# w_down of a hybrid block on one Trainium2 core: four Strassen pairs, another order of loads and transposes, results added by DMA

## The chip, the cores and the metric

The kernel runs on one core of one Trainium2 chip. The metric is the device time of one execution in microseconds. The weights lie in HBM in fp32; every matrix product runs on TensorE with fp32 operands split into two parts, and VectorE, ScalarE and GpSimd share the rest of the work.

## What is computed

One block of a streaming encoder, batch 1, sequence 256, width 2048, all in float32 (the reference, cut):

```python
u = rms_norm(x, norm_mix_w)
z = u @ w_in                       # HGRN2 q/f/i/out-gate, attention q/k/v, two branch gates
gate_a, gate_b = jnp.split(jax.nn.sigmoid(gates), 2, axis=-1)
merged = gate_a * (y_a @ w_branch_a) + gate_b * (y_b @ w_branch_b)
h = x + merged @ w_out             # w_out 2048 x 2048
u = rms_norm(h, norm_mlp_w)
h = h + jnp.square(jax.nn.relu(u @ w_up)) @ w_down     # w_up 2048 x 8192, w_down 8192 x 2048
return rms_norm(h, norm_final_w)
```

The recurrence (`y_a`) and the banded attention (`y_b`) come first and are not touched.

## The kernel before

**Products.** An fp32 weight tile is split into wh (ScalarE casts it, L89 in `split`) and wl (VectorE subtracts, L90); the activations are split in the same way beforehand. One k tile of 128 rows is then three matmuls of 128 x 512, hi·wh, hi·wl and lo·wh (`mm3`, L142–145).

**Loads.** SyncE's queue brings two k tiles of 512 columns at a time (`piece`, 512 KB) into a ring of 8 raw buffers. wh and wl have rings of 6 each (`BUFS`, `buf`). A buffer comes free when its last reader is done: a raw one after its last lo subtraction or sum, a wh or wl after its last matmul. Each queue runs in program order, moved by `tc.high_priority`.

**`gemm_s`.** It makes a block of 256 rows by 1024 columns out of 16 k tiles, in four PSUM banks c11, c12, c21, c22 (row half, column half). On r pairs of k tiles (k, k+4) it forms 7 products in place of 8 (Strassen's scheme in Winograd's form); the rest are plain pairs (`plains`, names r0_8, r1_8 and so on: column half and first k tile). Each Strassen pair saves 3 matmuls: 183 at r=3, 186 at r=2, where 192 would be plain. The pieces are W11, W12 (k tiles 0, 1; the two column halves) and W21, W22 (k tiles 4, 5); at r=3 the third pair's four tiles share two buffers X and Y. Sums of weights are made in place in the raw buffers (`add`, L700); sums of activations (S2, S4, S5, S7) are made once by `combos` (L587). A bank that takes over another bank's value starts from a ScalarE copy (L724); `more` (L729) adds or subtracts a token to or from a bank on VectorE. In products whose bank has never been written (`fresh`), a dummy matmul sets it up first (L740). The last pair of column half 1 is held over and runs inside the next product (`late`, `flush`).

**Order.** The products run in a fixed order: ga2, gb0, gb2 (gates, r=3), the branches, wo0 (r=3), wo2 (r=2), then for each of four quarters of the hidden width up{q}0, up{q}2 (r=3, up00 r=2), dn{q}0, dn{q}2 (r=3). Between them the activations are turned: `transpose4` (L106) makes four 128 x 128 transposes into a PSUM buffer (there are two), `split` reads it. A callback `between`, in the middle of the next product, does this for all blocks that are due (`turn`, `turns`, `h_blocks`); in the w_up and w_down products that is 16 transposes in three groups.

**Ends.** `done` gets each finished bank. For w_up it is relu and square on ScalarE (L947, L948). For w_down it is `out_of`: `evict` (L679) adds the bank to h on VectorE. In the last quarter the row sums of squares, the norm (L963–977) and the output DMAs follow; the last product (`tail`) holds three pairs back for column half 1, runs them for m=0, and then for m=1.

Of the kernel before, what the change touches and what calls it, by code (L numbers as in the profile page):

```python
# [16 lines left out]
P = 128  # L17
# [33 lines left out]
def tile_hybrid_block(  # L51
# [534 lines left out]
    def combos(lhs, what, home):  # L586

        a = []
        for m in range(NM):
            for j in range(2):  # L590
                t = tk.tile([P, R, P], F32, name=f"a{m}{j}_{what}", tag="t", bufs=TOK)
                x = lhs[j][:, :R, :, m * P:(m + 1) * P].bitcast(F32)
                nc.vector.tensor_tensor(t, x[:, :, 0, :], x[:, :, 1, :], op=ALU.add)
                a.append(t)
        a11, a12, a21, a22 = a
        s5 = a22
        nc.vector.tensor_tensor(s5, a21, a22, op=ALU.subtract)
        s7 = a21
        nc.vector.tensor_tensor(s7, a11, a21, op=ALU.subtract)
        s2 = a11  # L600
        nc.vector.tensor_tensor(s2, s5, a11, op=ALU.subtract)
        s4 = a12
        nc.vector.tensor_tensor(s4, a12, s2, op=ALU.add)
        made = {}
        for i, s in ((4, s4), (5, s5), (2, s2), (7, s7)):
            t = (tk if home == "a" else xp).tile([P, R, 2, P], F32R, name=f"S{i}_{what}", tag=f"S{i}{home}", bufs=1)
            split(t[:, :, 0, :], t[:, :, 1, :], s)
            made[i] = t
        return made
# [71 lines left out]
    def gemm_s(lhs, S, w, n0, what, done, r=R, kt0=0, between=None, fresh=False, tail=False):  # L681
# [4 lines left out]
        n1 = n0 + NC  # L686
        c = {}
        load = lambda name, *halves: piece(w, f"{what}{name}", *[(n, kt0 + k) for n, k in halves])
        W11 = load("11", (n0, 0), (n0, 1))
        if r == 3:  # L690
            X = load("x", (n0, 2), (n1, 6))
        W22 = load("22", (n1, 4), (n1, 5))
        W12 = load("12", (n1, 0), (n1, 1))
        if r == 3:
            Y = load("y", (n0, 6), (n1, 2))
        W21 = load("21", (n0, 4), (n0, 5))
# [16 lines left out]

        def of(m, jj):
            return lambda k: lhs_of(lhs, k + 4 * jj, m)

        def comb(i):
            return lambda k: [S[i][:, k, u, :] for u in range(2)]

        both = ((0, 0), (1, 1))  # L720
# [5 lines left out]

        def more(i, t, op):
# [4 lines left out]
        p = parts(W11, f"{what}p1")  # L732
        if r == 3:
            px = parts(X, f"{what}px")
        mm("11", of(0, 0), p, *both)
        if r == 3:
            mm("11", of(0, 0), px, (0, 2))
        c["21"] = bank(f"{what}c21")
        if fresh:
            nc.tensor.matmul(c["21"], lhs[0][:, 0, 0, 0:P], lhs[0][:, 0].rearrange("p u t -> p (u t)"), start=True, stop=False, skip_group_check=True)  # L740
        copy(c["21"], "11")
        p = parts(W22, f"{what}p3")
        add(W22[0], W12[0])
        add(W12[0], W11[0])
        mm("12", comb(4), p, *both)
        if r == 3:
            mm("12", comb(4), px, (1, 2))

        p = parts(W12, f"{what}p5")
        mm("22", comb(5), p, *both)  # L750
        if r == 3:
            add(half(X, 1), half(Y, 1))
# [6 lines left out]
        p = parts(W21, f"{what}p2")  # L759
        mm("11", of(0, 1), p, *both)  # L760
        add(W11[0], W22[0])
        flush()

        p = parts(W11, f"{what}p6")
        mm("21", comb(2), p, *both)
        if r == 3:
            add(half(X, 0), half(X, 1))
            px = parts(X, f"{what}px2")
            mm("21", comb(2), px, (0, 2))
        u1 = copy(token(f"u1_{what}"), "21")  # L770

        def plain(n, *ks):
            p = parts(load(f"r{n}_{ks[0]}", *[(n0 + n * NC, k) for k in ks]), f"{what}r{n}_{ks[0]}")
# [14 lines left out]
        left = [(k, k + 1) for k in range(2, KD, 2) if k != 4] if r == 2 else [(3, 7)] + [(k, k + 1) for k in range(8, KD, 2)]  # L788
        plains(1, left[0])
        more("12", u1, ALU.subtract)  # L790
        p = parts(W22, f"{what}p7")
        mm("21", comb(7), p, *both)
        if r == 3:
            mm("21", comb(7), px, (1, 2))
        u2 = copy(token(f"u2_{what}"), "21")
        add(W21[0], W11[0])
        early = left[1][1] // 4 < len(lhs)
        if early:
            plains(1, left[1])
        else:  # L800
            q = plain(0, *left[0])
            q(0)
        more("22", u2, ALU.subtract)
        p = parts(W21, f"{what}p4")
        mm("21", of(1, 1), p, *both)
        if r == 3:
            add(half(Y, 0), half(X, 0))
            mm("21", of(1, 1), parts(Y, f"{what}p4y", 0), (0, 2))
        if not early:
            q(1)  # L810
        if between:
            between()
# [5 lines left out]
        plains(0, *left[0 if early else 1:2])  # L818
        plains(1, *left[2 if early else 1:2])
        for n in range(2):  # L820
            plains(n, *left[2:-3])
        plains(0, *left[max(2, len(left) - 3):])
        end(0)
        if tail:
            held = [plain(1, *ks) for ks in left[-3:]]
            for m in range(NM):
                for p in held:
# [3 lines left out]
        plains(1, *left[-3:-1])  # L831

        def rest():
            plains(1, left[-1])
# [23 lines left out]
    def turn(n):  # L858
        mT.append(new_act(f"m{n}"))
        hi, lo = mT[n][:, :, 0, :], mT[n][:, :, 1, :]  # L860
        for m in range(NM):
            tp = transpose4(ga[n][m], f"m{n}{m}")
            split(hi[:, :, m * P:(m + 1) * P], lo[:, :, m * P:(m + 1) * P], tp)

    for n in range(4):
        for y, w, gate, what in ((ya, w_branch_a, ga[n], "ba"), (yb, w_branch_b, gb[n], "bb")):
# [3 lines left out]
            if what == "ba" and n:  # L870
                turn(n - 1)
# [11 lines left out]
    def h_blocks(n0):  # L883

        for n in (n0, n0 + 1):
            hT.append(new_act(f"h{n}"))
            hi, lo = hT[n][:, :, 0, :], hT[n][:, :, 1, :]
            for m in range(NM):
                t = h1[n][m]
                tp = transpose4(t, f"h{n}{m}")  # L890
                tmp = tk.tile([P, 4, P], F32, name=f"hw_{n}_{m}", tag="t", bufs=TOK)
                nc.vector.tensor_tensor(tmp, tp, bc(wmlp[:, 4 * n:4 * n + 4], 2, P), op=ALU.mult)
                split(hi[:, :, m * P:(m + 1) * P], lo[:, :, m * P:(m + 1) * P], tmp)
                nc.scalar.activation(token(f"hsq_{n}_{m}"), t, AF.Square, accum_out=ssq2[:, m, n:n + 1])
        if not n0:
            Sh.update(combos(hT, "h", "a"))
            return
        ssum2 = small.tile([P, NM], F32, name="ssum2", tag="ssum")
        nc.vector.tensor_reduce(ssum2, ssq2, axis=AX.X, op=ALU.add)
        rsqrt(rstd2, ssum2, D, NM)  # L900

    rstd2 = const.tile([P, NM], F32, name="rstd2")
    for n0 in (0, 2):
        for n in (n0, n0 + 1):
            for m in range(NM):
# [4 lines left out]
               between=lambda: h_blocks(0) if n0 else turn(3))  # L910
# [6 lines left out]
    for qd in range(NQ):  # L917
        last = qd == NQ - 1
        uT = []
        pend = []  # L920

        def turn():

            c, rs = pend.pop(0)
            uT.append(new_act(f"u{qd}{c}"))
            hi, lo = uT[-1][:, :, 0, :], uT[-1][:, :, 1, :]
            for m in range(NM):
# [99 lines left out]
```

## Time and profile before

| | us |
|---|---|
| median of 3 runs | 1425.47 (1424.73 to 1425.62) |
| the profiled execution | 1425.94 |
| its span | 1424.2 |

The profile is of one execution; its span runs from the first to the last instruction, and the execution's own time is 1.7 us longer. Its mean granted TensorE clock is 0.997 of full speed. In the table of windows a row gives a stretch (from:to, length), each engine's busy time and number of instructions in it, the granted clock, the busy share of the DMA engines and their GB/s. A timeline row gives start, duration, engine, line, operation, output and inputs, and in brackets the engine's idle time before it with what ended it. A row of groups ends with count, busy time, mean ns of one, and idle time by releaser. A row of DMA issues gives the count, the size and the median us from issue to landing.

### The profile page before, as it was taken

To read this page: it belongs to the slowest core of one execution; us is meant where nothing else is said; L and a number is where in the kernel's file an instruction comes from. 1 tells how busy PE (TensorE), PEld (TensorE's weight loads), DVE (VectorE), ACT (ScalarE), POOL (GpSimd) and SP (SyncE) were. 2 spreads that over 40 slices of the span, in tenths; PEclk is the share of its full clock that TensorE was granted. 3 is DMA by queue.
4 is the path that set the end of the run, shared out by engine and by line. 5 is a ranking of instruction groups with operands and counts; after the bars stand their busy time and mean duration, and the time that the engine had idled before them with its cause. 6 is when DMAs were issued, how large, how long until landed. Compare 5 with 4: busy or idle time off the path is not lost.

```text
span 1424.2 us, 18429 instructions
## 1 busy us (share of the span) xinstructions
PE 1404.4 (99%) x6629; PEld 1161.3 (82%) x6629; DVE 1153.6 (81%) x1522; ACT 852.8 (60%) x1108; POOL 36.8 (3%) x96
## 2 busy tenths in 40 slices
PE   9999999999999999999999999999999999999997
PEld 7888788878787888888888888888888888888886
DVE  7879887675758885688998988989888998889984
ACT  6766744464556664346656765566556775567753
POOL 2000101010000000000000000000000000000000
PEclk9999999999999999999999999999999999999999
DMA  9664344665556657666654576555576555667542
GB/s 329 221 194 149 130 162 134 189 177 164 166 177 222 202 192 227 197 203 222 207 182 134 192 232 215 181 196 167 188 235 233 183 168 169 236 222 237 179 152 98
DMA packets 122156, 272.89 MB, mean 192 GB/s; under 512 B 10176, under 2 KB 31424, under 8 KB 121680
## 3 DMA queue, kind: packets, MB, share of 16 engines
q1 hardware_dynamic: 119328, 264.80, 55.9%
q0 software_dynamic: 1584, 5.31, 1.4%
q10 hardware_dynamic: 1152, 1.60, 0.3%
q8 instruction: 52, 0.85, 0.2%
q14 instruction: 40, 0.33, 0.1%
HBM read 269.57 MB, written 2.10 MB: 191 GB/s over the span
## 4 chain that ended last, share of the span: by engine, by line
PE 81%; DVE 9%; DMA 4%; ACT 3%; issue 3%; POOL 0%; SPq 0%; POOLq 0%; ACTq 0%; DVEq 0%
PE acc_ak L171 2%; PE acc_aq L171 2%; PE acc_hf L171 2%; PE acc_hq L171 2%; PE ps L395 1%; PE acc_bb L143 1%; PE acc_av L143 1%; PE acc_ba L145 1%; PE acc_ba L144 1%; PE acc_bb L145 1%; PE acc_ba L143 1%; PE acc_av L144 1%; PE acc_bb L144 1%; PE acc_av L145 1%; PE acc_ak L170 1%
## 5 line engine op out<-in xcount | busy, mean ns | idle before, releaser
L171 PE MATMUL acc_hf<-act_x,wh_hf 128*128 128x512 f32 x128 | 47.5, 407 | 0.3 <-DVE wh_hf L89 0.3
L171 PE MATMUL acc_aq<-act_x,wh_aq 128*128 128x512 f32 x128 | 47.7, 407 | 0.0
L171 PE MATMUL acc_hq<-act_x,wh_hq 128*128 128x512 f32 x128 | 45.7, 397 | 0.0
L171 PE MATMUL acc_ak<-act_x,wh_ak 128*128 128x512 f32 x128 | 45.0, 397 | 0.0
L700 DVE TENSOR_TENSOR raw_up<-raw_up,raw_up 128x1024 f32<-128x1024 f32 x32 | 39.1, 1222 | 0.5
L700 DVE TENSOR_TENSOR raw_dn<-raw_dn,raw_dn 128x1024 f32<-128x1024 f32 x32 | 39.1, 1221 | 0.2
L90 DVE TENSOR_TENSOR wl_ga<-raw_ga,wh_ga 128x1024 fp32r<-128x1024 f32 x16 | 19.6, 1225 | 19.6 <-ACT wh_ga L89 17.9
L170 PE MATMUL acc_aq<-act_x,wl_aq 128*128 128x256 f32 x120 | 35.1, 293 | 0.0
L170 PE MATMUL acc_hf<-act_x,wl_hf 128*128 128x256 f32 x120 | 34.3, 286 | 0.0
L90 DVE TENSOR_TENSOR wl_av<-raw_av,wh_av 128x1024 fp32r<-128x1024 f32 x16 | 19.6, 1224 | 18.1 <-ACT wh_av L89 18.1
L170 PE MATMUL acc_ak<-act_x,wl_ak 128*128 128x256 f32 x120 | 33.6, 280 | 0.0
L170 PE MATMUL acc_hq<-act_x,wl_hq 128*128 128x256 f32 x120 | 33.6, 280 | 0.0
L90 DVE TENSOR_TENSOR wl_ba<-raw_ba,wh_ba 128x1024 fp32r<-128x1024 f32 x16 | 19.6, 1225 | 16.6 <-ACT wh_ba L89 16.6
L90 DVE TENSOR_TENSOR wl_bb<-raw_bb,wh_bb 128x1024 fp32r<-128x1024 f32 x16 | 19.6, 1223 | 14.7 <-ACT wh_bb L89 14.7
L89 ACT CAST wh_ba<-raw_ba 128x1024 fp32r<-128x1024 f32 x16 | 16.9, 1054 | 24.3 <-PE acc_ba L145 10.0
L89 ACT CAST wh_bb<-raw_bb 128x1024 fp32r<-128x1024 f32 x16 | 16.9, 1054 | 22.8 <-PE acc_ba L145 12.7
L89 ACT CAST wh_av<-raw_av 128x1024 fp32r<-128x1024 f32 x16 | 16.8, 1053 | 22.0 <-PE acc_av L145 12.4
L90 DVE TENSOR_TENSOR wl_aq<-raw_aq,wh_aq 128x1024 fp32r<-128x1024 f32 x16 | 19.6, 1224 | 12.5 <-ACT wh_aq L89 12.2
L89 ACT CAST wh_aq<-raw_aq 128x1024 fp32r<-128x1024 f32 x16 | 16.8, 1049 | 20.9 <-PE acc_aq L171 8.8
L171 PEld LDWEIGHTS acc_hf<-act_x,wh_hf 128*128 128x128 f32 x128 | 24.1, 188 | 5.7 <-DVE wh_hf L89 0.5
L171 PEld LDWEIGHTS acc_hq<-act_x,wh_hq 128*128 128x128 f32 x128 | 24.0, 188 | 5.4
L171 PEld LDWEIGHTS acc_ak<-act_x,wh_ak 128*128 128x128 f32 x128 | 23.9, 188 | 5.5
(1627 smaller groups left out, 5122.7 us busy)
## 6 DMA issues: line engine op xcount, KB each, us to landing
raw_up<-in_w_up_dram SPq DMA_DIRECT2D x32, 512.0 KB, 5.4
raw_dn<-in_w_down_dram SPq DMA_DIRECT2D x32, 512.0 KB, 5.3
raw_ga<-in_w_in_t_dram SPq DMA_DIRECT2D x20, 512.0 KB, 4.4
raw_hi<-in_w_in_n_dram SPq DMA_DIRECT2D x16, 512.0 KB, 3.9
raw_hg<-in_w_in_n_dram SPq DMA_DIRECT2D x16, 512.0 KB, 3.7
raw_aq<-in_w_in_t_dram SPq DMA_DIRECT2D x16, 512.0 KB, 4.4
raw_ak<-in_w_in_t_dram SPq DMA_DIRECT2D x16, 512.0 KB, 3.8
raw_av<-in_w_in_n_dram SPq DMA_DIRECT2D x16, 512.0 KB, 4.2
```

What stands on the lines that cost most here:

```text
L89: (copy or nc.scalar.copy)(hi, src)
L90: nc.vector.tensor_tensor(lo, src, hi.bitcast(F32), op=ALU.subtract)
L143: nc.tensor.matmul(acc, hi, wh, start=first, stop=False, skip_group_check=True)
L144: nc.tensor.matmul(acc, hi, wl, start=False, stop=False, skip_group_check=True)
L145: nc.tensor.matmul(acc, lo, wh, start=False, stop=last, skip_group_check=True)
L170: nc.tensor.matmul(acc[:, cb, 0:T], wl[:, c], r[:, 0, :], start=False, stop=False)
L171: nc.tensor.matmul(acc[:, cb, :], wh[:, c], r.rearrange("p u t -> p (u t)"), start=kt == 0, stop=kt == nkt - 1)
L395: nc.tensor.matmul(ps[:, m, :], klf[:, a * P:(a + 1) * P], qrf[:, a * 192:(a + 1) * 192], start=True, stop=True)
L700: nc.vector.tensor_tensor(dst, dst, t, op=ALU.add)
```

## The change

1. The w_down products take r=4. The pieces W11, W12, W22 and W21 have two loads each, so that they fill all 8 raw buffers; X and Y fall away there. `combos` gets the fourth tile's sums too (tiles S2m to S7m), and its blocks are copied by ScalarE from the transposes' PSUM buffers in place of being added up from hi and lo.
2. In all `gemm_s` products the loads come in the order of the ring, W11, (X), W12, (Y), W22, W21, and the products in the order c11 from W11, c22 from W12 + W11 with S5, c12 from W22 with S4, then W21. c12 starts from a copy of c22 (`begun`), where a token and a VectorE sum were; W12 is later remade as W22 − W11 (`less`). A `fresh` product has two dummy matmuls, not one. The held-over pair runs after the second product's copy.
3. Transposes are made one block at a time at fixed places (`point`, `steps`, `start`), not together in `between`.
4. In quarters 0 to 2 a w_down bank is copied to a token by ScalarE, and a DMA of GpSimd's queue adds the token to h (24 of 256 KB). The last quarter evicts as before.
5. The last product holds two pairs back for column half 1, and the held-over pair's load is issued at the end of its own product.

In all TensorE has 24 matmuls fewer in w_down and two more in ga2 and gb0; VectorE has 37 instructions fewer, ScalarE 64 more.

```diff
-    def combos(lhs, what, home):
+    def combos(lhs, what, home, blocks=None, n=R):
...
-        for i, s in ((4, s4), (5, s5), (2, s2), (7, s7)):
+        for two in ((5, s5), (4, s4)), ((2, s2), (7, s7)):
+            if n > R:
+                more = tk.tile([P, 2, 2, P], F32R, name=f"S{two[0][0]}m_{what}", tag="t", bufs=TOK)
...
-    def gemm_s(lhs, S, w, n0, what, done, r=R, kt0=0, between=None, fresh=False, tail=False):
+    def gemm_s(lhs, S, w, n0, what, done, r=R, kt0=0, steps=(), start=4, fresh=False, tail=False):
+        def point():
+            points[0] += 1
+            if points[0] > start and steps:
+                steps.pop(0)[1]()
+        groups = (0, 2) if r == 4 else (0,)
+        four = lambda name, n, k: [load(f"{name}{g}", (n, k + g), (n, k + g + 1)) for g in groups]
+        def less(dst, s, t):
+            with tc.high_priority(offset=2000):
+                nc.vector.tensor_tensor(dst, s, t, op=ALU.subtract)
+        def begun(i, j):
+            c[i] = bank(f"{what}c{i}")
+            if fresh:
+                nc.tensor.matmul(c[i], lhs[0][:, 0, 0, 0:P], lhs[0][:, 0].rearrange("p u t -> p (u t)"), start=True, stop=False, skip_group_check=True)
+            copy(c[i], j)
...
+        W11 = four("11", n0, 0)
+        W12 = four("12", n1, 0)
+        W22 = four("22", n1, 4)
+        W21 = four("21", n0, 4)
+        mms("11", of(0, 0), W11, "p1")
+        begun("21", "11")
+        for a, b in zip(W12, W11):
+            add(a[0], b[0])
+        mms("22", comb(5), W12, "p5")
-        more("12", copy(token(f"s5_{what}"), "22"), ALU.add)
+        begun("12", "22")
+        flush()
+        mms("12", comb(4), W22, "p3")
+        for a, b in zip(W22, W12):
+            add(a[0], b[0])
+        point()
+        mms("11", of(0, 1), W21, "p2")
+        for a, b, d in zip(W12, W22, W11):
+            less(a[0], b[0], d[0])
+        point()
+        mms("21", comb(2), W22, "p6")
         u1 = copy(token(f"u1_{what}"), "21")
+        point()
...
         plains(1, left[0])
         more("12", u1, ALU.subtract)
+        for a, b in zip(W21, W22):
+            add(a[0], b[0])
+        mms("21", comb(7), W12, "p7")
         u2 = copy(token(f"u2_{what}"), "21")
+        plains(1, left[1])
         more("22", u2, ALU.subtract)
+        mms("21", of(1, 1), W21, "p4")
+        point()
-        if between:
-            between()
...
+        held = max(2, len(left) - 3)
+        plains(0, *left[:held])
+        plains(1, *left[2:held])
+        plains(0, *left[held:])
         end(0)
         if tail:
-            held = [plain(1, *ks) for ks in left[-3:]]
+            ps = [plain(1, *ks) for ks in left[held:]]
...
+                if c < 2:
+                    blocks[m, c] = tk.tile([P, 4, P], F32, name=f"a{m}{c}_u{qd}", tag="t", bufs=TOK)
+                    nc.scalar.copy(blocks[m, c], tp)
...
         def out_of(m, n, acc, last=last):
             r = h1[n][m]
+            if not last:
+                t = token(f"y{qd}{n}{m}")
+                with tc.high_priority(offset=2000):
+                    nc.scalar.copy(t, acc)
+                nc.gpsimd.dma_start(r, t, accum_op=ALU.add)
+                return
             evict(r, acc)
...
-            gemm_s(uT, Su, w_down, n0 * NC, f"dn{qd}{n0}", lambda m, n, acc, n0=n0: out_of(m, n0 + n, acc), kt0=qd * KD,
-                   between=None if n0 else turns, tail=last and n0 == 2)
+            gemm_s(uT, Su, w_down, n0 * NC, f"dn{qd}{n0}", lambda m, n, acc, n0=n0: out_of(m, n0 + n, acc), r=4, kt0=qd * KD,
+                   steps=() if n0 else turns(2), start=0, tail=last and n0 == 2)
```

Beside these, the parts for r=3 (X and Y) follow the same new order, and `turns`, `turned` and `h_blocks` return lists of steps, one for each block.

More of the change, by code (lines that the diff above doesn't have):

```diff
@@ L729, in more @@
                 nc.vector.tensor_tensor(c[i], c[i], t, op=op)
[L732 removed]
+        W11 = four("11", n0, 0)
+        if r == 3:
+            X = load("x", (n0, 2), (n1, 6))
+        W12 = four("12", n1, 0)
+        if r == 3:
+            Y = load("y", (n0, 6), (n1, 2))
+        W22 = four("22", n1, 4)
+        W21 = four("21", n0, 4)
+        points[0] = -2
+        mms("11", of(0, 0), W11, "p1")
         if r == 3:
             px = parts(X, f"{what}px")
[L735 to L752 removed]
+            mm("11", of(0, 0), px, (0, 2))
+        begun("21", "11")
+        for a, b in zip(W12, W11):
+            add(a[0], b[0])
+        mms("22", comb(5), W12, "p5")
+        if r == 3:
             add(half(Y, 1), half(X, 0))
@@ L830, in gemm_s @@
             return
-        plains(1, *left[-3:-1])
+        plains(1, *left[held:-1])
+        while steps:
+            point()
+        raw = load(f"r1_{left[-1][0]}", *[(n1, k) for k in left[-1]])
         def rest():
-            plains(1, left[-1])
+            p = plain(1, *left[-1], raw=raw)
+            for m in range(NM):
+                p(m)
             end(1)
```

183 lines of the change are left out of this document (83 added, 100 removed).

## The prediction

> **What bounds the kernel now.** I read the page first, then one product's stretch in the table of windows, then the timelines of TensorE and VectorE there.
>
> ```profile
> span 1424.2 us, 18429 instructions
> ...
> PE 1404.4 (99%) x6629; PEld 1161.3 (82%) x6629; DVE 1153.6 (81%) x1522; ACT 852.8 (60%) x1108; POOL 36.8 (3%) x96
> ...
> PE 81%; DVE 9%; DMA 4%; ACT 3%; issue 3%; POOL 0%; SPq 0%; POOLq 0%; ACTq 0%; DVEq 0%
> ```
>
> PE is busy for nearly all of the span and carries 81% of the chain that ended last. Each row of the next view is one weight product, from its first matmul's start to that of the next: ga2, gb0, dn00, up12, dn10, dn12, dn20, dn30. Two rows of the timeline show how the bounds were taken.
>
> ```profile
> core 0: us, PE busy (x) PEld busy (x) DVE busy (x) ACT busy (x) POOL busy (x), PEclk, DMA share, GB/s
> 427.46:468.79 41.33, 39.62 (x174) 32.12 (x172) 36.97 (x37) 24.80 (x29) 0.00 (x0) 1.00 0.56 191
> 468.79:510.93 42.14, 41.99 (x185) 34.46 (x184) 33.50 (x33) 25.55 (x29) 0.00 (x0) 1.00 0.59 200
> 816.14:859.79 43.65, 43.60 (x201) 35.89 (x200) 37.03 (x39) 26.67 (x33) 0.00 (x0) 1.00 0.59 193
> 942.75:986.14 43.39, 43.39 (x201) 35.88 (x199) 40.06 (x48) 31.47 (x41) 0.00 (x0) 1.00 0.60 194
> 986.14:1030.20 44.06, 43.87 (x201) 35.81 (x199) 37.02 (x39) 26.67 (x33) 0.00 (x0) 1.00 0.57 191
> 1030.20:1071.68 41.48, 41.48 (x185) 34.35 (x183) 35.70 (x37) 23.57 (x26) 0.00 (x0) 1.00 0.62 203
> 1156.57:1200.37 43.80, 43.66 (x200) 35.81 (x199) 37.02 (x39) 26.58 (x33) 0.00 (x0) 1.00 0.57 192
> 1326.72:1370.54 43.82, 43.68 (x201) 35.80 (x199) 37.10 (x40) 27.64 (x36) 0.00 (x0) 1.00 0.58 192
> ```
> ```profile
> 1030.20 0.39 PE L143 MATMUL acc_dn12c<-wh_dn12p,act_u 128*128 128x512 f32 x1
> ...
> 1071.68 0.39 PE L143 MATMUL acc_up20c<-wh_up20p,act_h 128*128 128x512 f32 x1
> ```
>
> The product dn12 issues 183 matmuls and no transposes in 41.48 us: 0.2267 us each (0.39 is the length of one in the pipeline, not the pitch), with PE busy throughout and VectorE for 35.70. So it is issue-bound, at a granted clock of 1.00. up12 adds 16 transposes without idle time: 43.39 − 41.48 = 1.91 us. The four w_down products with transposes take 43.65, 44.06, 43.80 and 43.82: above 43.39 by 0.26, 0.67, 0.41 and 0.43, in all 1.8 us of stalls. ga2's 172 matmuls want 38.99 us and take 41.33 (2.3 of stalls); gb0's 184 want 41.71 and take 42.14 (0.4). That is all a better order can win back in these rows.
>
> **1. Fewer matmuls.** Eight w_down products go from 183 to 180: 24 × 0.2267 = −5.44. ga2 and gb0 get a second dummy matmul: +0.45. Net −5.0, on the path, as PE sets it.
>
> **2. Sums started by a copy.** In place of a copy to a token and a VectorE sum, c12 starts from a ScalarE copy of c22.
>
> ```profile
> 433.57 0.50 PE L143 MATMUL acc_ga2c<-wh_ga2p,S_x 128*128 128x512 f32 x1 [1.64 <-ACT wh_ga2p L89]
> ```
> ```profile
> 988.65 0.58 ACT L724 COPY acc_dn10c<-acc_dn10c 128x512 f32<-128x512 f32 x1
> ```
>
> ga2's stall at 433.57 waits for a cast that stands behind VectorE sums; the new order wants only W11 and W12 there. What is late next is the copy: matmul tail 0.39 plus about 0.5 before c12's first matmul, since ga2 has no held-over pair to run meanwhile. I take 1.0 of the 2.3 as left: −1.3 (ends: −2.3 if the dummy's own time covers it, 0 if the first sums are as late as now). gb0's 0.4 goes. In wo0 no held-over pair covers the copy either: +0.2. Together −1.5.
>
> **3. The chain on VectorE in a w_down product.** With four pairs all eight raw buffers are held by W11 to W21, and VectorE has 14 lo subtractions and 8 sums for the 84 matmuls of the seven products. Its pitch is read from an unbroken stretch of dn10, and a load's time from the list of DMA issues there:
>
> ```profile
> 985.85 1.22 DVE L90 TENSOR_TENSOR wl_dn10p<-raw_dn,wh_dn10p 128x1024 fp32r<-128x1024 f32 x1
> ...
> 993.80 1.22 DVE L90 TENSOR_TENSOR wl_dn10r<-raw_dn10r,wh_dn10r 128x1024 fp32r<-128x1024 f32 x1
> 994.93 0.70 DVE L729 TENSOR_TENSOR acc_dn10c<-acc_dn10c,s_dn 128x512 f32<-128x512 f32 x1
> 995.53 1.22 DVE L90 TENSOR_TENSOR wl_dn10p<-raw_dn,wh_dn10p 128x1024 fp32r<-128x1024 f32 x1
> ```
> ```profile
> L89 ACT CAST wh_dn10r<-raw_dn10r 128x1024 fp32r<-128x1024 f32 x9 | 9.4, 1054 | 4.7 <-DVE wl_dn10p L90 2.1 <-DMA raw_dn10r<-in_w_down_dram 1.7 <-PE acc_dn10c L145 0.9
> ```
> ```profile
> raw_dn10r<-in_w_down_dram SPq DMA_DIRECT2D x8, 512.0 KB, 5.3
> ...
> raw_dn12r<-in_w_down_dram SPq DMA_DIRECT2D x1, 512.0 KB, 3.7
> ```
>
> From 985.85 to 994.93 eight operations of 1024 columns start 1.135 us apart; one of 512 takes 0.60 to the next. Let a product begin at 0. The first cast of W22 needs a wh buffer of the ring of six that the last pair of the previous product frees just then, so it ends at about 0.39 + 1.05, and VectorE's lo of it starts at 1.5. From there the order of the changed kernel puts 20 operations of 1024 (lo's of W22, W21, p6, r1_8, p7, r1_10, p4 and two of r0, four sums, two `less`) ahead of the u lo that frees a PSUM buffer for the third transposition: it starts at 1.5 + 20 × 1.135 = 24.2 and ends at 24.9. TensorE reaches that transposition after 100 matmuls in dn00 and dn30 (22.7), 102 in dn20 (23.1) or 103 in dn10 (23.35), and two groups at 0.5 each (1.91/16 × 4): 23.7, 24.1 and 24.35. VectorE then has two more lo's before c12 −= u1, which ends at 27.75; TensorE wants c12 for r1_10 at 26.0 to 26.2 in dn00 and dn30, 27.35 in dn10. So TensorE waits 1.6 us in dn00 and dn30 (for c12), 0.8 in dn20 and 0.55 in dn10 (for the PSUM buffer). Sum 4.5 against 1.8 before: **+2.7**. Below, the old 1.8 could vanish as well (−1.8), if VectorE enters the product earlier than the ring says; above stands the load of r1_8, a rival below. In the products without transposes the same chain reaches r1_8 at 15.1 and TensorE at 16.3: 16.25 against 16.3, no stall, and no slack.
>
> **4. Transposes one block at a time.** Eleven products (wo0, wo2, up00, four of up, four of w_down) get one group more. Around 1013.12 four transposes and the change back cost 0.50 where 4 × 1.91/16 = 0.48 is the mean in groups of three; a change between kinds is therefore some 0.05: 11 × 0.05 = **+0.6** (0 to 1.1, at twice that).
>
> ```profile
> 1013.12 0.66 PE L106 MATMUL tp_u<-ident,r 128*128 128x128 f32 x4
> 1013.53 0.48 PE L145 MATMUL acc_dn10c<-wh_dn10r,act_u 128*128 128x512 f32 x1
> 1013.85 0.39 PE L143 MATMUL acc_dn10c<-wh_dn10r,act_u 128*128 128x512 f32 x1
> ```
>
> **5. Results added by DMA.** 24 VectorE sums of 0.69 go, 24 ScalarE copies of 0.58 and 24 DMAs of 256 KB from GpSimd's queue come. VectorE's saving lies outside the chain of step 3, so I count nothing for it; ScalarE is 60% busy. No one waits for the landing until the last quarter's evictions. No row shows an accumulating DMA; the nearest is a load of h.
>
> ```profile
> h<-in_x_dram POOLq DMA_DIRECT2D x8, 256.0 KB, 4.4
> ```
>
> Two of them fly from about 10 to 14.4 in the products dn02, dn12, dn22, beside r1_8's load, issued when `less` ends at 9.5. At 3.7 us it lands at 13.3 and its cast ends at 14.3, before VectorE is there (15.1); at 5.3 it ends at 15.95, 0.85 late. Times three: 0 to 2.6; I take **+1.0**. An accumulating DMA that is several times as slow still holds only its own token.
>
> **6. The tail.** These are the last rows of h, the last VectorE and ScalarE work, and the last outputs.
>
> ```profile
> 1411.15 0.69 DVE L679 TENSOR_TENSOR h<-acc_dn32c,h 128x512 f32<-128x512 f32 x1 [1.91 <-PE acc_dn32c L145]
> ...
> 1413.69 0.49 DVE L975 TENSOR_SCALAR h<-h,rstd 128x512 f32<-128x512 f32 x1 [0.71 <-POOL rstd L96]
> 1414.09 0.75 DVE L973 SCALAR_TENSOR_TENSOR h<-h,rstd,wf 128x512 f32<-128x512 f32 x1
> ...
> 1415.23 0.69 DVE L679 TENSOR_TENSOR h<-acc_dn32c,h 128x512 f32<-128x512 f32 x1 [0.40 <-PE acc_dn32c L145]
> ```
>
> Now the two last blocks end 18 matmuls apart (1411.15 and 1415.23: 4.08). Two held pairs make it 12 matmuls, 2.72. The m=0 block's L975 and L973 start 2.54 and 2.94 after its eviction and stand ahead of the last eviction on VectorE, which can start 3.60 after: 0.88 late, **+0.9** (0 if the hardware ran it first, which the order excludes; the same 0.9 at most).
>
> **Sum.** −5.0 − 1.5 + 2.7 + 0.6 + 1.0 + 0.9 = −1.3. The profiled execution took 1425.94 us (span 1424.2), 0.5 above the median 1425.47; −1.3 from the median is 1424.2. With the smaller uncertainties of steps 2, 4 and 5 its own range is 1421.5 to 1427.5.
>
> **Rivals.**
> *(a) TensorE stays the only bound.* VectorE's chain starts before 1.5, or scheduling hides it, so that w_down stalls as now; no contention, no late eviction: −5.0 − 1.5 + 0.6 = −5.9, 1419.6; if the old stalls of 1.8 go too, 1417.8. For it: PE 99% and VectorE below it in every row. Against: VectorE's share is a mean, and step 3's chain has 22 operations for 84 matmuls, 25.0 us against 19.0.
> *(b) r1_8's load decides, slower.* W11's buffer comes free at 9.5, and nothing loads before. In before a load of that kind is on the chain of waits at 6.40:
>
> ```profile
> 1002.52 6.40 DMA raw_dn10r<-in_w_down_dram
> ```
>
> At the median of 5.3, VectorE, in order, waits for r1_8 from 14.0 to 16.0 in the four products with transposes, and all of step 3 slips: 1.6 more each than at 3.7; the other four lose 0.85. That is 6.4 + 3.4 − 1.0 counted = +8.8: 1433.0; at half of it 1428.6. It decides from a landing of 3.4 us with transposes, 4.4 without. Against it: nothing else loads then, and a load alone took 3.7.
> *(c) Operations on VectorE do not overlap in their ends.* Then each takes its whole 1.22 in the chain: 20 × 0.085 = 1.7 in each of four products, 13 × 0.085 = 1.1 in the others, +11: 1435. The rows at 985.85 to 994.93 speak against it. The Trainium skill, page "VectorE: DVE Perf Modes", section "The DRAIN you can't avoid", says that the next operation does not start until the pipeline is empty. Here starts are 1.135 us apart at a length of 1.22, so the trace doesn't agree.
> That the change doesn't do what it says has no room: its instructions hold 180 matmuls for each w_down product and the 24 DMAs.
>
> **Chances.** Forecast 0.45, (a) 0.31, (b) 0.21, (c) 0.03. About 0.2% (2.85 us) is what a measurement can tell: faster means below 1422.6, slower above 1428.3. Faster: (a) and 0.11 of the forecast, 0.42. Slower: most of (b), (c), 0.02 of the forecast: 0.25. The rest, 0.33, within. The range goes from (a)'s lower part to the middle of (b): 1418.0 to 1431.0.
>
> **What would show it.** Rows of w_down without transposes at 40.81 us (180 × 0.2267): step 1 and no stall; with transposes 43.3 to 44.4: step 3; below 43 is (a), 45 and more is (b), with TensorE's idle time put down to casts of r1_8. ga2 near 40.3. A gap of about 0.9 ahead of the last eviction, with VectorE busy: step 6. The forecast is wrong if TensorE idles in products that the change hardly touches, or the granted clock falls below 1.00 behind the longer waits.

## The result and the profile after

| | us |
|---|---|
| before, median of 4 runs beside it | 1425.1 (1424.4 to 1425.62) |
| after, median of 4 runs | 1433.32 (1432.29 to 1434.01) |
| ratio after / before | 1.0057, 95% interval 1.0044 to 1.0069 |
| the profiled execution of after | 1434.01, span 1432.3 |

The change makes the kernel 8.2 us slower, by 0.57%. The forecast was 1424.2 with a range of 1418.0 to 1431.0, so the time lies above the range. The page of after has these rows, which answer to those of before:

```profile
span 1432.3 us, 18448 instructions
...
PE 1403.7 (98%) x6607; PEld 1155.6 (81%) x6607; DVE 1146.5 (80%) x1485; ACT 890.6 (62%) x1172; POOL 58.0 (4%) x120
...
PE 82%; DVE 6%; DMA 6%; ACT 2%; issue 2%; POOL 0%; SPq 0%; POOLq 0%; DVEq 0%; ACTq 0%
```

They say little: TensorE is busy for as long as before and the span is 8 us longer, so TensorE idles; and the share of DMA in the chain has gone from 4% to 6%. The table of windows, cut again from first matmul to first matmul, tells where (ga2, gb0, dn00, up12, dn10, dn12, dn20, dn30):

```profile
427.49:467.52 40.03, 39.59 (x174) 32.32 (x173) 32.29 (x33) 24.55 (x28) 0.00 (x0) 1.00 0.59 198
467.52:509.56 42.04, 42.04 (x186) 34.65 (x185) 32.47 (x32) 25.64 (x29) 0.00 (x0) 1.00 0.59 200
814.96:861.35 46.39, 43.55 (x198) 35.05 (x196) 38.10 (x36) 30.20 (x36) 1.79 (x2) 1.00 0.54 187
945.08:988.92 43.84, 43.68 (x200) 35.88 (x199) 38.50 (x45) 34.24 (x49) 0.00 (x0) 1.00 0.57 192
988.92:1034.22 45.30, 43.65 (x197) 35.11 (x196) 38.01 (x36) 29.80 (x36) 1.70 (x2) 1.00 0.55 192
1034.22:1076.06 41.84, 41.39 (x181) 33.63 (x180) 37.03 (x36) 26.53 (x30) 3.40 (x4) 1.00 0.75 226
1161.70:1206.11 44.41, 43.37 (x197) 35.05 (x196) 37.91 (x36) 30.04 (x36) 1.70 (x2) 1.00 0.56 196
1332.89:1378.19 45.30, 43.53 (x198) 35.05 (x196) 39.69 (x39) 30.50 (x38) 0.00 (x0) 1.00 0.52 186
```

The gates win as forecast: ga2 41.33 to 40.03, gb0 42.14 to 42.04. The w_down products with transposes, which issue 3 matmuls fewer, take 46.39, 45.30, 44.41 and 45.30, where 43.65, 44.06, 43.80 and 43.82 were: +6.1. dn02, dn12 and dn22, the ones without, give back 1.0 in place of gaining 2.0. The granted clock is 1.00 in all rows, so it has no part in this. The rest of the 8: seven w_up products together +2.0 (up12 above: +0.45), the last product −0.4, the tail +0.8.

The waits of TensorE, engine by releaser, in dn00 (815 to 861), dn10 (989 to 1034), dn20 (1162 to 1206) and dn30 (1333 to 1378), with us of idle time in total, times and the longest:

```profile
PE acc_dn00c L143 <- ACT u_dn L744: 1.5, 1, 1.5
PE tp_u L106 <- DVE act_u L90: 1.2, 1, 1.2
PE acc_dn00c L144 <- DVE wl_dn00r L90: 0.2, 1, 0.2
```
```profile
PE acc_dn10c L143 <- DVE acc_dn10c L756: 0.9, 1, 0.9
PE acc_dn10c L143 <- ACT u_dn L744: 0.7, 2, 0.4
```
```profile
PE acc_dn20c L143 <- ACT u_dn L744: 0.8, 1, 0.8
PE tp_u L106 <- DVE act_u L90: 0.3, 1, 0.3
```
```profile
PE acc_dn30c L143 <- ACT u_dn L744: 1.0, 1, 1.0
PE tp_u L106 <- DVE act_u L90: 0.6, 1, 0.6
PE acc_dn30c L144 <- DVE wl_dn30r L90: 0.2, 1, 0.2
```

The second row of dn00 is the wait that the prediction priced: a transposition waits until VectorE has read the PSUM buffer; the first row of dn10, for c12, is the other one. The first row of dn00, which all four products have, is one that it hadn't: the copy u2 on ScalarE. Counted from start to start of the matmuls the waits cost more than their idle time (835.70 to 837.57 below is 1.87, with a pitch of 0.23, for 1.49 of idle time). The timeline of ScalarE, TensorE and VectorE shows how it comes about in dn00:

```profile
832.91 1.05 ACT L89 CAST wh_dn00p<-raw_dn 128x1024 fp32r<-128x1024 f32 x1
835.99 1.05 ACT L89 CAST wh_dn00r<-raw_dn00r 128x1024 fp32r<-128x1024 f32 x1 [2.02 <-DMA raw_dn00r<-in_w_down_dram]
836.94 0.58 ACT L744 COPY u_dn<-acc_dn00c 128x512 f32<-128x512 f32 x1
```
```profile
835.70 0.39 PE L145 MATMUL acc_dn00c<-wh_dn00p,S2m_u 128*128 128x512 f32 x1
837.57 0.50 PE L143 MATMUL acc_dn00c<-wh_dn00p,act_u 128*128 128x512 f32 x1 [1.49 <-ACT u_dn L744]
```
```profile
837.07 1.23 DVE L90 TENSOR_TENSOR wl_dn00r<-raw_dn00r,wh_dn00r 128x1024 fp32r<-128x1024 f32 x1 [0.17 <-ACT wh_dn00r L89]
839.79 1.23 DVE L90 TENSOR_TENSOR wl_dn00r<-raw_dn00r,wh_dn00r 128x1024 fp32r<-128x1024 f32 x1 [1.50 <-ACT wh_dn00r L89]
840.94 0.68 DVE L90 TENSOR_TENSOR act_u<-tp_u,act_u 128x512 fp32r<-128x512 f32 x1
```

TensorE starts p7's last matmul at 835.70 and has p4 next, which writes the bank that u2 is to be copied from. (In the program r1_10 stands between the two; in the order that runs, p4 has come ahead of it.) The copy itself is short, but on ScalarE's queue it stands behind the cast of an r0 pair, which waits for its load. On VectorE the u lo (the lo subtraction of a turned block, which reads the PSUM buffer of its transposes) stands behind the lo's of the same r0 pairs (1.50 us of idle time at 839.79), and starts at 840.94, 26.0 us into the product, where the prediction had 24.2. These loads come in a burst; the instructions on r0 and r1 pairs of dn00, taken by their tile, list the time from issue to landing (least, median, most):

```profile
DMA to landing us min/median/max: 3.8/6.1/7.5
```

The first is r1_8's, at 3.75 us, as forecast; the later ones, for the most part issued 1.1 us apart as VectorE frees a buffer, take up to twice as long.

### The profile page after: what moved, and what is told of

It is laid out like the page before. It is cut to its first block, busy times and chain, and to the rows that moved or that the text cites. A ratio compares the mean times of both kernels' runs of the same rounds, so it can differ in the third digit from the quotient of the medians.

```text
span 1432.3 us, 18448 instructions
## 1 busy us (share of the span) xinstructions
PE 1403.7 (98%) x6607; PEld 1155.6 (81%) x6607; DVE 1146.5 (80%) x1485; ACT 890.6 (62%) x1172; POOL 58.0 (4%) x120
## 4 chain that ended last, share of the span: by engine, by line
PE 82%; DVE 6%; DMA 6%; ACT 2%; issue 2%; POOL 0%; SPq 0%; POOLq 0%; DVEq 0%; ACTq 0%
PE acc_ak L171 2%; PE acc_aq L171 2%; PE acc_hf L171 1%; DMA raw_hf<-in_w_in_t_dram 1%; PE ps L395 1%; PE acc_hq L171 1%; PE acc_bb L144 1%; PE acc_ba L144 1%; PE acc_av L145 1%; PE acc_ba L145 1%; PE acc_bb L143 1%; PE acc_bb L145 1%; PE acc_ba L143 1%; PE acc_av L143 1%; PE acc_av L144 1%
## 5 line engine op out<-in xcount | busy, mean ns | idle before, releaser
L711 DVE TENSOR_TENSOR raw_dn<-raw_dn,raw_dn 128x1024 f32<-128x1024 f32 x48 | 58.1, 1218 | 3.1 <-DMA raw_dn<-in_w_down_dram 2.8
L711 DVE TENSOR_TENSOR raw_up<-raw_up,raw_up 128x1024 f32<-128x1024 f32 x24 | 29.3, 1222 | 14.5 <-DMA raw_up<-in_w_up_dram 14.2
L1000 POOL DMA_DIRECT2D h<-y x24 | 20.5, 853 | 477.8 <-ACT y L999 477.1
L171 PEld LDWEIGHTS acc_hf<-act_x,wh_hf 128*128 128x128 f32 x128 | 24.2, 189 | 6.2 <-DVE f L179 1.4
```

The source lines that it names most:

```text
L171: nc.tensor.matmul(acc[:, cb, :], wh[:, c], r.rearrange("p u t -> p (u t)"), start=kt == 0, stop=kt == nkt - 1)
L1000: nc.gpsimd.dma_start(r, t, accum_op=ALU.add)
```

## The experiments

Parts of the runs ahead of the first changed product differ by some 4 us between kernels whose code is the same there (ga2 begins at 425.2 to 429.1), so products are compared beside the totals. The ratios are against runs of before beside each group; their medians lay between 1425.35 and 1426.12. Two theories stood after the result: **L**, that holding all eight raw buffers makes loads stand still and then come in a burst; and that something else does it (VectorE's chain, the order of the queues, the DMA sums). The kernels e1, e5, e6 and e12 also make the activations' sums for a fourth pair only where a product uses them.

### Which edit: e1, e2, e3, e4

e1_r3:
```diff
-  ..., r=4, kt0=qd * KD,
+  ..., r=3, kt0=qd * KD,
```


> The changed kernel with w_down back at three Strassen pairs (183 matmuls each, pieces X and Y as in w_up); order, transposes by block, the DMA sums and the tail stay. Theory L (with four pairs all eight raw buffers are held until VectorE's sums free them, so loads stand still for 9.5 us and then come in a burst at the full bandwidth, landing after 6 to 8 us): w_down's products go back to about 41.5 and 43.4 to 44 us, the whole to about 1426 us: 1425.1 less 1.4 in ga2 and gb0, plus 0.8 in the tail and some 1.5 in transposes and DMA sums. Rival P (the transposes by block, the DMA sums or ScalarE's order make the stalls): they stay, and 5.4 us of matmuls come back: 1433 or more.

Measured: 1421.93 (before 1426.12), ratio 0.9967, interval 0.9956 to 0.9977. With three pairs, the other edits together are a gain of 4 us; the tail's is not among them, for with three pairs five plain pairs are left and the last product holds three of them back again. dn10 and dn12 of this kernel:

```profile
983.72:1027.12 43.40, 43.40 (x201) 35.91 (x199) 35.13 (x36) 28.35 (x35) 1.70 (x2) 1.00 0.64 206
1027.12:1068.60 41.48, 41.48 (x185) 34.35 (x183) 32.55 (x32) 25.36 (x29) 3.40 (x4) 1.00 0.72 229
```

There is no stall left at all: the 1.8 us of before are gone, and four groups of transposes cost what three did (43.40 − 41.48 = 1.92). So the loss is tied to the fourth pair, and by 4 us more than theory L had put it: it had 0.8 for the tail, which is 9.01 us here against 9.86 in after, and 1.5 for transposes by block and DMA sums, which cost nothing here.

e2_evict:
```diff
-            if not last:
-                t = token(f"y{qd}{n}{m}")
...
-                nc.gpsimd.dma_start(r, t, accum_op=ALU.add)
-                return
             evict(r, acc)
+            if not last:
+                return
```


> The changed kernel with w_down's results added by VectorE in all quarters, no accumulating DMAs. Theory: two accumulating DMAs share the bandwidth with r1_8's load in dn02, dn12 and dn22, which landed in 5.26 us there and in 3.75 where none flew; without them the 0.6 to 0.8 us wait for r1_8's lo in each of these goes: 1431 us. Rival: the load is late by itself, or VectorE's 24 sums of 0.6 us cost as much in its chain: 1433 to 1434.

Measured: 1431.42, ratio 1.0043 (1.0028 to 1.0058): 1.9 us less than after, the total that the theory gave, but not by its route. dn02, dn12 and dn22 fell by 0.36, 0.36 and 0.07, by less than forecast; in the profiled execution the products with transposes fell by 1.6 together, those of w_up rose by 1.1, and 1.6 lay ahead of ga2. In dn12 r1_8's load landed in 3.96 us, but `less` stood behind two evictions on VectorE, and the load was issued 1.2 us later in the product (10.7 after its start, against 9.5). So the load is faster without the DMAs (3.96 against 5.26), but taking them away mostly moves the wait.

e3_halfload:
```diff
+        if what[:2] == "dn" and what[4] == "r":
+            nc.sync.dma_start(raw[:, :NC], w[n0 // NC, k0 // 4, :, k0 % 4, :])
+            return raw, None
...
+        if turned is None:
+            dst = [t.rearrange("p (a n) -> p a n", a=2) for t in made]
+            src = bc(raw[:, :NC], 1, 2)
```


> The changed kernel, but the plain pairs of w_down (r0 and r1) load only their first k tile, 256 KB in place of 512, and the casts and lo subtractions read it twice, so that the work of the engines stays and half of these bytes go; the second k tile of each such pair is left out of the result. Theory L: the loads land in under 5 us, ScalarE no longer stands at a cast with u2's copy behind it; what stays is at most step 3's 4.5 us in the products with transposes: 1423 to 1427. Rival V (VectorE's chain of 25 us against 19 on TensorE sets it): 1431 or more.

Measured: 1430.54, ratio 1.0036 (1.0022 to 1.0050). In dn10 the first six loads of plain pairs landed in 2.9 to 3.5 us, where after had 3.8 to 7.7. The products without transposes fell to 40.80 us, 180 × 0.2267, without any stall. Those with transposes kept 45.80, 44.87, 45.21 and 45.48, 181.4 in all as before the edit. So theory L holds for the one kind and fails for the other; though here VectorE's order shifted as well (a sum for the next product, waiting for its load, came ahead of a u lo), which alone would not let this run decide.

e4_raw9:
```diff
-    TOK = 17
+    TOK = 15
-    BUFS = {"raw": (6, 2), "wh": (4, 2), "wl": (4, 2)}
+    BUFS = {"raw": (6, 3), "wh": (4, 2), "wl": (4, 2)}
```


> The changed kernel with nine raw buffers in place of eight; two token buffers fewer (15) make the room. Theory L: r1_8's load is issued some 9 us earlier and every load behind it one buffer earlier; the 0.6 to 0.8 in each product without transposes goes, and 1 us or more in each with them: 1426 to 1429. Rival V: one buffer changes nothing at VectorE's chain: 1432 to 1434.

Measured: 1428.3, ratio 1.0018 (1.0008 to 1.0027), 5 us less than after. dn02, dn12 and dn22 took 40.80 each, the last product 43.71. Those with transposes took 47.09, 43.59, 44.56 and 44.60: not settled by a buffer. dn00 is the longest for a second reason: behind its wait of 1.96 us for u2's copy the granted clock was 0.50 for 3.4 us.

```profile
838.53:841.94 3.41, 3.41 (x12) 2.73 (x11) 2.44 (x3) 1.77 (x2) 0.00 (x0) 0.50 1.00 396
```

### Which products: e5, e6, e7

e5_n2, e6_n2r9 (which adds e4's edit to e5) and, as the second cut, e7_n0:
```diff
-  ..., r=4, kt0=qd * KD,
+  ..., r=4 if n0 and not last else 3, kt0=qd * KD,
...
-  ..., r=4, kt0=qd * KD,
+  ..., r=3 if n0 else 4, kt0=qd * KD,
```


> Four Strassen pairs only in dn02, dn12 and dn22, the products without transposes; three pairs in the other w_down products, the rest as in the changed kernel. Theory: the cost of four pairs is in the products with transposes (VectorE's chain, with the u lo's and the loads on it); in those without, the 0.7 us of matmuls saved is about lost again to r1_8's late load: 1421 to 1423, that is within 1 us of three pairs everywhere (1421.9). Rival: four pairs cost in every product: 1425 or more.

> The same with nine raw buffers and 15 token buffers. Theory: r1_8's load has its own buffer, so the three products take 40.81 us (180 x 0.2267) and the others lose nothing: 1419.5 to 1420.5. Rival: the smaller token ring makes new waits: 1422 or more.

> Four Strassen pairs only in dn00, dn10, dn20 and dn30, the products with transposes; three in the others. Theory: these four take some 45.3 us in place of the 43.40 they have with three pairs, so 1421.9 + 4 x 1.9 = 1429 to 1431. Rival (the load on all queues over a whole quarter is what counts): about half of the changed kernel's loss, 1427 or less.

Measured: e5 1425.35, ratio 1.0 (0.999 to 1.0009); e6 1426.14, ratio 1.0 (0.9991 to 1.0009); e7 1432.97, ratio 1.0044 (1.0028 to 1.0061). e7 bears out that four pairs hurt where the transposes are, and by more than the 1429 to 1431 expected: its four products took 185.0 us, where 181.2 were expected. dn00 alone took 49.22, with ScalarE's cast of an r0 pair waiting 4.38 us for its load and u2's copy behind it; TensorE waited 3.85 us for that copy, and behind the wait its granted clock was 0.50 for 3.4 us:

```profile
836.68 1.04 ACT L89 CAST wh_dn00r<-raw_dn00r 128x1024 fp32r<-128x1024 f32 x1 [4.38 <-DMA raw_dn00r<-in_w_down_dram]
837.63 0.58 ACT L744 COPY u_dn<-acc_dn00c 128x512 f32<-128x512 f32 x1
```
```profile
839.49:842.90 3.41, 3.41 (x10) 2.59 (x9) 2.75 (x3) 1.19 (x2) 0.00 (x0) 0.50 1.02 378
```

e5 and e6 missed. In e5 the three products took 41.85, 41.66 and 41.96, so four pairs cost 0.2 to 0.5 there against three, and up12 took 44.61. In e6 they took 40.80, as expected, but up12 took 46.73: on VectorE a lo and two sums of weights (the last, for the next product's Y, 0.29 us idle for its load) had come ahead of a sum of the activations; ScalarE's next cast waited 3.14 us for that sum, a u copy stood behind it, and TensorE waited 2.71 us for the copy. The order of a queue is made anew with every edit, and a product that the edit doesn't touch can pay.

### Which order: e8 to e12

e8_pool:
```diff
         for a, b in zip(W21, W22):
+            if r == 4 and start == 0 and n0 % 1024 == 0 and steps0:
+                nc.gpsimd.tensor_tensor(a[0], a[0], b[0], op=ALU.add)
...
```


> The changed kernel, with the two sums W21 += W22 of the products with transposes on GpSimd in place of VectorE; the order on VectorE changes with it, the u lo's come earlier and r1_10 ahead of p4. Theory V (VectorE's chain is what those four products wait for): two operations of 1.135 us less on the chain, 1.5 us or more in each: 1425 to 1429. Rival L (the loads set it, the chain only follows): 1432 or more. GpSimd's own time for such a sum is not known; if it is over some 4 us, p4 waits for it and the time rises.

Measured: 1449.23, ratio 1.0164 (1.0149 to 1.0180), a miss of 20 us. GpSimd took 3.27 us for a sum, and each sum held VectorE up by 2.2 us (see the end): 4.4 us a product, against 2.3 that the two sums had cost VectorE itself. The products became longer by 3.3 to 4.5. TensorE's only wait in dn10 is for a u lo on VectorE, and behind it the granted clock was 0.53 for 3.55 us:

```profile
PE tp_u L106 <- DVE act_u L90: 4.3, 1, 4.3
```
```profile
1008.93:1012.48 3.55, 3.55 (x14) 2.96 (x14) 3.55 (x4) 1.05 (x2) 0.00 (x0) 0.53 0.83 262
```

So VectorE's chain is on the path of e8. TensorE's order is another one too (the third group of transposes comes at 17.9 us of dn10, at 25.7 in after), so between V and L the run does not decide for after.

e9_noturn:
```diff
             def one(c, m):
+                if c > 1:
+                    if not m:
+                        uT.append(uT[c - 2])
+                    return
```


> The changed kernel, but dn00, dn10, dn20 and dn30 turn nothing: blocks 0 and 1 of the hidden activations stand for 2 and 3, so their transposes and splits are left out (7.7 us of TensorE at 1.92 a product). Theory: in these four products the late work is VectorE's order and ScalarE's queue around the turned blocks (the u lo's behind r0's, u2's copy behind r0's cast, p4 right behind p7 because r1_10 comes too late); without them a product is like dn02 and takes 41.4 to 42.0 us: 1417.5 to 1420. Rival L (the burst of loads alone): they stay at 43.4 or more (45.3 less 1.92): 1425 or more.

Measured: 1417.33, ratio 0.9938 (0.9922 to 0.9953). The four products took 40.80 each, with no stall; 41.4 to 42.0 was expected. The loads are no faster than in after: 4.4 to 8.8 us in dn00. So the burst is not enough by itself; what is late hangs on the turned blocks, whose work this kernel leaves out.

e10_ulo:
```diff
+                with tc.high_priority(offset=20000):
                     split(hi[:, :, m * P:(m + 1) * P], lo[:, :, m * P:(m + 1) * P], tp)
```


> The changed kernel with the splits of the turned blocks of u at a higher priority, so that VectorE does their lo's some ten operations earlier; no work is added or left out. Theory: TensorE's waits for the PSUM buffers of the transposes (1.2, 0.9, 0.3 and 0.6 us) go, the waits for u2's copy stay: 1430 to 1431.5. Rival (the delay only moves to the lo's that are now later): 1433 or more.

Measured: 1424.03, ratio 0.9992 (0.9982 to 1.0002), far better than either theory. The four products took 42.7 us each, no stall. The waits for u2's copy went as well, which the expectation had staying: with the blocks turned early, TensorE's order has r1_10 between p7 and p4, and the copy is covered. up12 took 45.71, a new wait.

e11_u2first:
```diff
+        if behind is not None:
+            with tc.high_priority(offset=2000):
+                nc.scalar.copy(made[0][:, 0:1], behind[:, 0:1])
...
-            p = parts(raw, f"{what}r{n}_{ks[0]}")
+            p = parts(raw, f"{what}r{n}_{ks[0]}", behind=u2s[0] if u2s and not n else None)
```


> The changed kernel; in the four products with transposes each r0 cast on ScalarE is put behind u2's copy by a copy of one column out of u2 ahead of it (16 copies of 128x1). On VectorE the r0 lo's then come behind the u lo's. Theory: u2's copy no longer stands behind a cast that waits for a load, so TensorE's wait for it falls from 0.7 to 1.5 us to the copy's own 0.4 to 0.7, and the waits for the transposes' buffers go: 43.5 to 44 us a product, 1426.5 to 1429. Rival (bandwidth: r0's data aren't there anyway): the wait moves to the r0 pairs, 1432 or more.

Measured: 1430.08 (1426.62 to 1431.05), ratio 1.0024 (1.0011 to 1.0037). The four products took 43.85, 44.33, 43.74 and 43.83, near the expected 43.5 to 44; dn12 lost 1.0 to a new wait, and the total is 1 us over the expected one. TensorE's only wait in dn00 is the copy's own length, as here p4 still stands right behind p7:

```profile
PE acc_dn00c L143 <- ACT u_dn L749: 0.7, 1, 0.7
```

Together: 181.4 us for the four products in after, 175.75 with the queues' order mended (e11), 170.8 with TensorE's as well (e10). So 5.6 us go when the u lo's and u2's copy no longer stand behind r0 pairs, and 5.0 more when TensorE's order has r1_10 ahead of p4 and the transposes early as well. No run changes TensorE's order alone, so this division is one of differences.

e12_mix (e6 with the steps of `point` and `plain` at a higher priority):


> Four Strassen pairs in dn02, dn12 and dn22 only, nine raw buffers, 15 tokens, and the steps that turn blocks and make the activations' sums at a higher priority, so that on VectorE these sums no longer stand behind a sum of weights that waits for its load (3.1 us in up12 where they did). Theory: 40.81 in the three products, up12 back at 43.4 to 43.9, the rest as with three pairs everywhere: 1419 to 1421. Rival: the new order makes another wait of that kind: 1423 or more.

Measured: 1423.83, ratio 0.9987 (0.9978 to 0.9996): the rival's time, but not its mechanism. up12 came back to 44.53 only. wo0, up10, up20 and up30 took 1.1 to 1.3 us more than in e6, without a wait of TensorE, because each had 8 more transposes in it; dn00, dn10, dn20 and dn30 had 8 fewer and took 0.8 to 1.0 less. The move costs 1.3 us in all.

### Both remedies: e13, e14, e15

e13_ulo_dn is e10 for the blocks with c > 1 alone; e14_ulo_raw9 adds e4's edit; e15_last3 adds `r=3 if last and n0 else 4`.


> The changed kernel, with the higher priority for the splits of the turned blocks in the four w_down products with transposes alone. No work is added or left out. Theory O (the order: VectorE's u lo's stand some ten operations too late, so that transposes wait for their PSUM buffers and p4 stands right behind p7 with nothing to cover u2's copy): these products go from 46.39, 45.30, 44.41 and 45.30 to 42.7 us, up12 stays at 43.85, in all 10.6 us less: 1422.5 to 1423.5. Rival (the gain with all u splits came from w_up's share): 1427 or more.

> The same with nine raw buffers and 15 tokens. Theory: the other part of the loss is r1_8's raw buffer in the products without transposes; they go to 40.80 us, 3.6 us in all with dn32: 1418.5 to 1420. Rival: the smaller token ring or another order makes new waits (3.1 us in up12 of one kernel had that cause): 1421.5 or more.

> The same with three pairs in the very last product, so that three plain pairs are held back for its m=1 half: 0.65 us more of matmuls and stalls there, 0.85 less behind the last matmul, as the tail of 9.86 us with two held pairs and 9.0 with three says: 0.2 us less than with nine raw buffers alone, 1418 to 1420. Rival: the tail's difference has another cause, 1420 or more.

Measured: e13 1422.46, ratio 0.9978 (0.9969 to 0.9987); e14 1419.32, ratio 0.9956 (0.9942 to 0.9969); e15 1419.48, ratio 0.9955 (0.9941 to 0.9968). All three came out inside the expected times or within 0.1 us of them. The first u lo of dn10 starts 11.64 us into the product in e13; in after it was 24.58. Its row, then dn10 of e13 with all its work and no stall (after took 45.30), and dn10 and dn12 of e14:

```profile
995.64 0.68 DVE L90 TENSOR_TENSOR act_u<-tp_u,act_u 128x512 fp32r<-128x512 f32 x1
```
```profile
984.00:1026.69 42.69, 42.69 (x197) 35.36 (x196) 37.92 (x36) 29.80 (x36) 1.73 (x2) 1.00 0.58 202
```
```profile
982.25:1025.01 42.76, 42.76 (x198) 35.28 (x197) 37.93 (x36) 29.91 (x36) 1.70 (x2) 1.00 0.61 203
1025.01:1065.81 40.80, 40.80 (x182) 33.78 (x181) 37.16 (x36) 26.95 (x30) 3.40 (x4) 1.00 0.76 233
```

VectorE is as busy as in after (38.0), TensorE now all the time, and the loads of dn10 still land in 4.0 to 7.3 us: with the same burst, the order decides whether TensorE stalls. In e15 the tail is 8.77 us against 9.85, and the last product 44.46 against 43.71: as the expectation said in kind, with no difference in the total that these runs can tell. e14 and e15 are 0.4% faster than before, with four pairs throughout or nearly.

## Why the prediction was wrong, by its own steps

**Step 1, fewer matmuls: right.** 180 × 0.2267 = 40.81; e14 has 40.80 in each product without transposes, and the 5.4 us are there to be had.

**Step 2, sums started by a copy: right.** ga2, gb0 and wo0 together changed by −1.30 − 0.11 + 0.12 = −1.29, with the two dummies (+0.45) in it; −1.5 + 0.45 was forecast.

**Step 3, the chain on VectorE: this failed.** It gave 4.5 us of stalls in the four products with transposes; there were 181.4 − 4 × (40.80 + 1.92) = 10.5, so +8.7 against before in place of +2.7. The pitch of 1.135 and r1_8's load (issued at 9.48 in dn00, landed 3.75 later) held, and the start nearly (1.3 in dn00 for 1.5). The waits that the step priced stayed within its 4.5: 2.1 us of idle time for the PSUM buffer and 0.9 for c12 in the four products; the one that it did not have, for u2's copy, was the largest, 4.0. What failed is what the step left out. It took every operation behind r1_8 as ready in time, though each needs its load, and the loads behind r1_8's landed after 4.7 to 7.5 us in dn00; and it looked for TensorE's waits at two places alone, the PSUM buffer and c12. It did not ask what stands behind an r0 cast on ScalarE (u2's copy), nor what TensorE has between p7 and p4 (in after, nothing, or in dn10 a single matmul). e10 and e13, which add and remove no work, show it: the stalls go when the u lo's come first. A chain of 22 operations against 84 matmuls isn't the limit that the step made of it, as most of it isn't needed as early as it stands in the queue.

**Step 4, transposes by block: too high.** +0.6 was taken; e1 shows 0. The w_up products that make sums for four pairs cost 0.26 more (43.67, 43.41 with three: up32 in e13 and e5); the step had no term for the fourth tile's sums. up10 and up20, which make no such sums, cost 0.28 and 0.24 more as well (41.76 and 41.72, 41.48 each in e1). Where in the products that goes wasn't tried.

**Step 5, results by DMA: the size was off.** The stalls in dn02, dn12 and dn22 were 41.97 + 41.84 + 41.63 − 3 × 40.80 = 3.0, where 1.0 was taken. r1_8's load landed in 5.26 us in dn12 beside a DMA sum that took 7.0. But e2 gets only 0.8 of it back without the DMAs, and e4 all of it with a ninth buffer: the load has no buffer until `less` is done, which the step named, and put at the edge of a stall. e3, where the load is half as large and landed in 3.8 us in dn12, gets all of it back too, so an earlier load and a shorter one both do.

**Step 6, the tail: right.** +0.9 was forecast. The eviction that waited, in after:

```profile
1422.69 0.75 DVE L1013 SCALAR_TENSOR_TENSOR h<-h,rstd,wf 128x512 f32<-128x512 f32 x1
...
1423.36 0.68 DVE L687 TENSOR_TENSOR h<-acc_dn32c,h 128x512 f32<-128x512 f32 x1
```

It starts when VectorE is done with the m=0 rows, and from TensorE's last matmul to the end it is 9.86 against 9.04: +0.82. With three pairs held back again it is 9.01 (e1).

**The rivals.** (a) described what e1 and e14 reach, not the change as it was made. (b) gave 1433.0, near the measured time, but by another route: its load of r1_8 with 2 us of delay in the products with transposes didn't occur; its 0.85 in the others did in kind: TensorE's waits for a plain pair's lo in dn02, dn12 and dn22 were 0.61, 0.45 and 0.53. A number that comes out right bears out no mechanism. It was the loads behind r1_8 that were late, with u2's copy behind their casts on ScalarE's queue. (c) was rightly put low; a row of VectorE's timeline in dn00 that holds two operations of 1024:

```profile
818.65 2.35 DVE L90 TENSOR_TENSOR wl_dn00p<-raw_dn,wh_dn00p 128x1024 fp32r<-128x1024 f32 x2
```

Two take 2.35 us, 1.22 and a pitch of 1.13, where two lengths would be 2.44. The Trainium skill, page "VectorE: DVE Perf Modes", section "The DRAIN you can't avoid", says that the next operation does not start until the pipeline is empty, and adds that one which is not held starts earlier. The prediction took up the first half alone; the trace shows the second, by 0.09 us.

## What to carry to other kernels

When a change fills a ring of buffers completely, ask for each load behind it, not for the first alone, when its buffer comes free and which other work stands behind its cast on an in-order queue; the sum of busy times won't show it. Work that frees a scarce buffer (here the lo's of the turned blocks) belongs ahead of bulk work that is only early, and a priority on the splits of 16 blocks was worth 11 us. Before a good idea is dropped for a loss, undo its parts one by one: here the idea was sound, and its order was not.

## What the runs showed of the hardware that was not expected

GpSimd's elementwise work holds up VectorE's. In e8, on VectorE, in dn10, beside a sum on GpSimd from 997.19 to 1000.45 and one from 1001.66 to 1004.92:

```profile
996.97 1.22 DVE L712 TENSOR_TENSOR raw_dn<-raw_dn,raw_dn 128x1024 f32<-128x1024 f32 x1
998.10 3.43 DVE L90 TENSOR_TENSOR wl_dn10p<-raw_dn,wh_dn10p 128x1024 fp32r<-128x1024 f32 x1
1001.45 4.55 DVE L717 TENSOR_TENSOR raw_dn<-raw_dn,raw_dn 128x1024 f32<-128x1024 f32 x2
```
```profile
997.19 3.26 POOL L838 TENSOR_TENSOR raw_dn<-raw_dn,raw_dn 128x1024 f32<-128x1024 f32 x1 [83.06 <-DVE wl_dn10p L90]
1001.66 3.26 POOL L838 TENSOR_TENSOR raw_dn<-raw_dn,raw_dn 128x1024 f32<-128x1024 f32 x1 [1.22 <-DVE wl_dn10p L90]
```

The VectorE operation that runs when GpSimd's begins keeps its 1.22 us; the next one takes 3.43 and ends 1.08 after GpSimd's, and two that take 2.35 otherwise take 4.55. Each GpSimd sum costs VectorE 2.2 us, about what two of its own operations do. The Trainium skill, page "GPSIMD Engine Reference", section "1. Specifications", says that GpSimd shares its SBUF interfaces with VectorE, with contention from VectorE instructions that have two SBUF inputs; the trace agrees, and gives the size.

A long wait of TensorE can cost it clock as well. Behind waits of 1.96 us (e4, dn00), 3.85 (e7, dn00) and 4.35 to 4.46 (e8, the four products with transposes) the granted clock was 0.5 for 3.4 us, or 6.8 in two products of e8, and in dn00 of e7 matmuls started 0.43 us apart in place of 0.23. It stayed at 1.00 behind 1.49 us in dn00 of after and 2.71 in up12 of e6, so the length of the wait alone does not say whether it falls.

A DMA that adds 256 KB to h landed in 3.2 to 3.5 us at the end of dn12 in after; in the middle one took 7.0, beside another such DMA and loads of weights.
